# First block's down-projection of a hybrid encoder layer as seven block products, weight differences on GpSimd and activation sums by accumulating transfers

## The chip, the cores and the metric

The kernel runs on one core of a Trainium2 chip. A core has TensorE (PE; its weight loads are listed as PEld), VectorE (DVE), ScalarE (ACT), GpSimd (POOL), SyncE (SP), and 16 DMA engines that all queues share. The engines run side by side, each through its own instructions in a fixed order. The metric is the device time of one execution in microseconds (us); less is better.

## The reference

One layer of a streaming encoder over 2048 prompt rows and 128 sample rows of width 1024, all in fp32: a combined input projection, chunk-band attention and an mLSTM side by side (the mixers), an output projection with a residual, and then the part that the change touches, a feed-forward network with a causal depthwise convolution of width 3:

```python
def conv_ffn(h, buf, w_up, w_conv, b_conv, w_down):
    S = h.shape[1]
    u = h @ w_up
    ext = jnp.concatenate([buf.astype(u.dtype), u], axis=1)
    y = b_conv
    for j in range(CONV_W):
        y = y + ext[:, j:j + S] * w_conv[j]
    gate, up = jnp.split(y, 2, axis=-1)
    out = (jax.nn.gelu(gate, approximate=True) * up) @ w_down
    return out, ext[:, S:]

    ffn, new_buf = conv_ffn(rms_norm(x, norm_g[2]), conv_buf, w_up, w_conv, b_conv, w_down)
    x = x + rms_norm(ffn, norm_g[3])
```

`w_up` is 1024 x 5632, `w_down` 2816 x 1024. The 17 row tiles of 128 are the 16 of the prompt and one of the sample.

## The kernel before

**Numbers.** Every fp32 matrix is split into a high part that TensorE takes exactly and a remainder: ScalarE copies the high part (L1309), VectorE subtracts it (L1310), and `mm3` (L104 to L106) makes three matmuls, high by high, high by low, low by high.

**Stages.** The mixers come first: 14 groups of columns of the input projection for each of two halves of the rows (`seq`, `GROUPS`). Between the units of a group, a pump (`pump`) steps attention and mLSTM along. The output projection follows. Then the feed-forward network runs over three blocks of rows, `FBLOCKS`: six tiles, six tiles, five tiles. For each block the up-projection goes over 22 column pairs f (gate and up, 128 columns each), and then the down-projection over the same 22 f as its inner dimension.

**Up-projection.** It already runs as seven block products in place of eight (Strassen's scheme in Winograd's form), with sums of the weights and of the activations. For the first block the weight sums are made on the way: for each f, `load_quads` loads four quads of 128x512 (`wu`), VectorE makes four sums of them (`ws`, L1326), and GpSimd stores those to DRAM (`wsd`, L1328) for the later blocks. Quads are 11 tiles in rotation, so a new load by SyncE waits until an old quad has been split or stored. GpSimd also copies two columns of history into each `uu` or `ug` (from `halo`, L1495) and out of it (L1500), which the convolution on VectorE (L1504, L1505) reads. The result of one f, g (L1654), is gate times up for all rows of the block.

**Down-projection.** `FAST` names the blocks that take it as seven products, here the second and the third. Rows are paired (tiles 0 to 2 with 3 to 5), and so are f (f with f + 11, index k of 11) and the output columns (two halves of 512). `SEQUENCE` names for each product an activation sum (A11, A12, S2, S1, S3, S4, A22), a block or difference of the weights, and which of two sets of three accumulators it adds to. A product is 11 k x 3 tiles x 3 matmuls of 512 columns: 99. `store_a` makes the sums for those blocks: plain stores of A11, A12, A22; S1 by an accumulating transfer; S3, S2 and S4 by three subtractions on VectorE (L1597) and a store each. The weight differences (`wtd`) are made during the first block's down-projection: `folds`, stepped once per k, loads four quads of `w_down` on ScalarE's queue, subtracts four times on VectorE (L1181) and stores them through GpSimd (L1186).

The first block itself takes the plain way: g goes to DRAM (`gd`, L1662), and two passes, one per half of the output columns, each load 22 blocks of weights (`load_down`) and 22 of g, with six accumulators: 2 x 22 x 6 x 3 = 792 matmuls. Between the passes the accumulators are copied out (L1394). During either kind of down-projection the next block's activations are normalised, transposed (L1107) and summed.

**Order.** Each engine's order is fixed when the kernel is built, by a list scheduler with a timeline of its own. Instructions under `keep_in_program_order` hold their order among themselves.

## Time and profile before

| | |
|---|---|
| median of 3 runs | 2769.21 us (2767.95 to 2771.8) |
| the profiled execution | 2768.76 us |
| its span, first to last instruction | 2767.0 us |
| mean granted TensorE clock | 0.996 |
| mixers and output projection | 0 to 1315.9 us |
| first block: up, down | 321.9 us, 200.0 us |
| second block: up, down | 318.7 us, 173.6 us |

The page lists busy time by engine, the chain of work that ended last, and groups of instructions by source line; a group's row has its count, busy time, mean length in ns, and the idle time of its engine just before it with what ended that. Views of the trace give busy time in chosen stretches (the stretch, its length, busy time with the number of instructions for PE, PEld, DVE, ACT and POOL, then granted clock, DMA share and GB/s), waits (who waited for whom: total, times, longest), and single instructions in order of time (start, length, engine, line). In a view by tile or line the three lengths are minimum, median and maximum in ns. Line numbers are those of the kernel before; `wuh`, `wul` are the split weights, and an L with a number is a line.

### The profile page before, as it was taken

The page shows a single profiled execution, that of the slowest core. Times are in us where ns is not written, and L with a number is a line of the kernel's source. Part 1 is how long each engine was busy: PE and PEld are TensorE (multiplying, and loading weights), DVE is VectorE, ACT ScalarE, POOL GpSimd, SP SyncE. Part 2 cuts the span into 40 slices and gives each one's busy share as a digit, 9 for nine tenths or more (in the row PEclk, how much of TensorE's full clock was granted, in tenths as well). Part 3 has the DMA queues.
Part 4 walks back from the last instruction along what each step waited for, and adds up shares of the span by engine and source line. Part 5 has one row for each costly group of instructions (what it writes and reads, how often), then busy time and mean ns, then how long its engine had stood idle before and what let it go on. Part 6 is the DMA issues. An engine that isn't in the chain of part 4 may idle for free.

```text
span 2767.0 us, 47747 instructions
## 1 busy us (share of the span) xinstructions
PE 2693.8 (97%) x16422; PEld 2520.4 (91%) x16422; DVE 1943.2 (70%) x3615; ACT 1438.5 (52%) x2918; POOL 654.3 (24%) x1271
## 2 busy tenths in 40 slices
PE   8999999999999999999999999999999999999998
PEld 7899999998899998878999998789999878999976
DVE  5344455646546668766989987668888876998956
ACT  4355555645356666543545455445455665554554
POOL 1000010211100002344434322123332212455401
PEclk9999999999999999999999999999999999999999
DMA  5534355556554456355645559866785777787775
GB/s 184 158 116 139 105 161 173 158 155 210 166 180 143 140 168 195 108 167 196 229 153 187 168 189 326 300 222 205 230 239 174 248 235 231 222 257 230 247 261 178
DMA packets 326017, 536.11 MB, mean 194 GB/s; under 512 B 60002, under 2 KB 159806, under 8 KB 325646
## 3 DMA queue, kind: packets, MB, share of 16 engines
q1 hardware_dynamic: 248382, 393.82, 45.7%
q0 software_dynamic: 32464, 93.87, 10.4%
q10 hardware_dynamic: 44928, 45.37, 5.1%
q8 instruction: 129, 2.11, 0.3%
q14 instruction: 114, 0.93, 0.1%
HBM read 383.28 MB, written 159.08 MB: 196 GB/s over the span
## 4 chain that ended last, share of the span: by engine, by line
PE 53%; DVE 3%; DMA 2%; issue 1%; POOL 1%; ACT 1%; DVEq 0%; POOLq 0%; SPq 0%; ACTq 0%
PE uec L104 6%; PE uec L105 6%; PE uec L106 6%; PE dn L106 4%; PE dn L105 4%; PE dn L104 4%; PE ua L106 3%; PE ua L105 3%; PE ua L104 3%; PE wo L106 2%; PE wo L104 2%; PE wo L105 2%; PE dnm L106 2%; PE dnm L105 2%; PE dnm L104 2%
## 5 line engine op out<-in xcount | busy, mean ns | idle before, releaser
L104 PE MATMUL uec<-B,wuh 128*128 128x384 f32 (+1 forms) x720 | 236.1, 328 | 4.1 <-DVE uu L1644 4.1
L105 PE MATMUL uec<-B,wuh 128*128 128x384 f32 (+1 forms) x720 | 235.3, 327 | 0.0
L106 PE MATMUL uec<-B,wul 128*128 128x384 f32 (+1 forms) x720 | 234.1, 327 | 0.0
L1309 ACT CAST wuh<-wu 128x512 fp32r<-128x512 f32 x255 | 141.7, 618 | 108.8 <-PE uec L105 100.9
L1310 DVE TENSOR_TENSOR wul<-wu,wuh 128x512 fp32r<-128x512 f32 x255 | 165.5, 685 | 4.0 <-DMA x2d<-mx 2.8
L405 DVE CUSTOM_DVE_ANT_0 tmp<-s,nb 128x640 f32<-128x640 f32 (+4 forms) x128 | 94.4, 737 | 95.1 <-PE s L395 93.5
L104 PE MATMUL vo<-wi_h,hT 128*128 128x256 f32 x544 | 155.1, 285 | 0.6 <-DVE mt L211 0.6
L106 PE MATMUL vo<-wi_h,hT 128*128 128x256 f32 x544 | 155.6, 286 | 0.0
L105 PE MATMUL vo<-wi_l,hT 128*128 128x256 f32 x544 | 154.8, 285 | 0.0
L104 PEld LDWEIGHTS uec<-B,wuh 128*128 128x128 f32 x720 | 135.2, 188 | 6.6 <-DVE uu L1644 5.5
L104 PE MATMUL qk<-hT,wi_h 128*128 128x384 f32 (+1 forms) x384 | 128.5, 335 | 7.3 <-ACT qk_st L236 5.9
L105 PEld LDWEIGHTS uec<-B,wuh 128*128 128x128 f32 x720 | 135.4, 188 | 0.3
L106 PEld LDWEIGHTS uec<-B,wul 128*128 128x128 f32 x720 | 135.1, 188 | 0.0
L418 DVE TENSOR_TENSOR ptl<-pt,pth 128x640 fp32r<-128x640 f32 (+4 forms) x128 | 93.6, 737 | 55.9 <-ACT pth L417 54.8
L406 ACT ACTIVATE tmp<-tmp,mn 128x640 f32<-128x640 f32 (+4 forms) x128 | 97.6, 762 | 67.0 <-DVE mn L405 62.9
L1310 DVE TENSOR_TENSOR wdl<-wdr,wdh 128x512 fp32r<-128x512 f32 x198 | 125.1, 685 | 7.3 <-ACT wdh L1309 7.0
L1310 DVE TENSOR_TENSOR al<-ar,ah 128x768 fp32r<-128x768 f32 (+2 forms) x94 | 70.9, 764 | 82.5 <-ACT ah L1309 81.0
L105 PE MATMUL qb<-hT,wi_h 128*128 128x384 f32 (+1 forms) x384 | 127.9, 333 | 0.0
L105 PE MATMUL qk<-hT,wi_h 128*128 128x384 f32 (+1 forms) x384 | 127.5, 332 | 0.0
L106 PE MATMUL qk<-hT,wi_l 128*128 128x384 f32 (+1 forms) x384 | 127.2, 331 | 0.0
L106 PE MATMUL qb<-hT,wi_l 128*128 128x384 f32 (+1 forms) x384 | 127.2, 331 | 0.0
L104 PE MATMUL qb<-hT,wi_h 128*128 128x384 f32 (+1 forms) x384 | 127.1, 331 | 0.0
(445 smaller groups left out, 9373.0 us busy)
## 6 DMA issues: line engine op xcount, KB each, us to landing
wu<-in_w_up SPq DMA_DIRECT2D x220, 256.0 KB, 4.9
wu<-wsd SPq DMA_DIRECT2D x176, 256.0 KB, 4.8
wdr<-in_w_down SPq DMA_DIRECT2D x110, 256.0 KB, 5.0
wi_raw<-in_w_in SPq DMA_DIRECT2D x52, 512.0 KB, 4.0
wsd<-ws POOLq DMA_DIRECT2D x88, 256.0 KB, 3.6
wdr<-wtd SPq DMA_DIRECT2D x88, 256.0 KB, 5.3
gr<-gd SPq DMA_DIRECT2D x39, 384.0 KB, 6.0
kraw<-kTd SPq DMA_DIRECT2D x112, 128.0 KB, 3.2
```

The costliest lines, as they stand in the source:

```text
L104: nc.tensor.matmul(out, ah, bh, start=start, stop=False, skip_group_check=onto)
L105: nc.tensor.matmul(out, ah, bl, start=False, stop=False, skip_group_check=onto)
L106: nc.tensor.matmul(out, al, bh, start=False, stop=stop, skip_group_check=onto)
L405: nc.vector.tensor_tensor_reduce(o_, s_, b_, 1.0, 3e38, ALU.add, ALU.min, accum_out=mn)
L406: nc.scalar.activation(tmp[:, :n], tmp[:, :n], AF.Exp, bias=mn, scale=-1.0, accum_out=rsum[:, i % 4, hh:hh + 1])
L418: nc.vector.tensor_tensor(s.ptl[:, sl, qc], ptv, s.pth[:, sl, qc], op=ALU.subtract)
L1309: nc.scalar.copy(h, r)
L1310: nc.vector.tensor_tensor(l, r, h, op=ALU.subtract)
```

## The change

`FAST` takes in the first block, whose order of f becomes 0, 11, 1, 12 and so on. The weight differences must then be ready before its down-projection: `folds` now runs in the mixers, from the second group of the first half on, one step per unit, with loads, arithmetic and stores all on GpSimd. The signs of two differences are turned, and in the later blocks those of two sums with them.

The activation sums of the first block are not made on VectorE. `send_a` stores A11, A12, A22 and S1 as before, and makes S3, S2, S4 in DRAM, in one tensor with three slots (`sums`): ScalarE negates A21 (for f under 11) or A22, and GpSimd's queue stores the negated A21 into three slots, adds A11 to all three, the negated A22 to two and A12 to one. The steps for one f wait in the list `due` and are taken one per later f.

```diff
-FAST = (1, 2)
+FAST = (0, 1, 2)
+FOLD_AT = 1
...
+    sums = dt_([P, 3, NK, 384], "sums")
+    for i, what in enumerate(("S3", "S2", "S4")):
+        ad[0, what] = sums[:, i]
...
+                    keep(nc.gpsimd.dma_start(live[k, x], I["w_down"][k][:, x * 512:(x + 1) * 512]))
...
+        for k in range(NK):
+            load(k, (0, 1))
+            yield
+            load(k, (2, 3))
+            yield
+            yield
+            yield
             a, b, c, d = [live[k, x] for x in range(4)]
+            for o, x, y, op in ((a, b, a, ALU.subtract), (b, c, b, ALU.subtract), (c, a, c, ALU.subtract),
+                                (d, d, c, ALU.add)):
+                keep(nc.gpsimd.tensor_tensor(o, x, y, op=op))
                 yield
+            store(k, range(4))
+            yield
...
+            if half == 0 and gi >= FOLD_AT:
+                next(fold, None)
...
+        def next_due():
+            for step in due.pop(0) if due else ():
+                step()
+
+        def send_a(f, gt):
...
+            while len(due) < 4:
+                due.append([])
+            next_due()
+            neg = []
+
+            def negate():
+                neg.append(spare_tile(f"neg{b}_{f}")[:, :384])
+                keep(nc.scalar.activation(neg[0], gt[:, 384:768], AF.Copy, scale=-1.0))
+
+            def spread(src, lo, **how):
+                keep(send(sums[:, lo:3, k, :], src.unsqueeze(1).broadcast_to([P, 3 - lo, 384]), **how))
+
+            if f < NK:
+                send(ad[b, "A11"][:, k, :], gt[:, 0:384])
+                send(ad[b, "S1"][:, k, :], gt[:, 384:768])
+                due[0] += [negate, lambda: spread(neg[0], 0)]
+                due[1] += [lambda: spread(ad[b, "A11"][:, k, :], 0, accum_op=ALU.add)]
+            else:
+                send(ad[b, "A12"][:, k, :], gt[:, 0:384])
+                send(ad[b, "A22"][:, k, :], gt[:, 384:768])
+                send(ad[b, "S1"][:, k, :], gt[:, 384:768], accum_op=ALU.add)
+                due[0] += [negate]
+                due[1] += [lambda: spread(neg[0], 1, accum_op=ALU.add)]
+                due[2] += [lambda: spread(ad[b, "A12"][:, k, :], 2, accum_op=ALU.add)]
...
-            for o, x, y in ((s3, a11, a21), (s2, a22, s3), (s4, a12, s2)):
-                nc.vector.tensor_tensor(o, x, y, op=ALU.subtract)
+            for o, x, y, op in ((s3, a11, a21, ALU.subtract), (s2, s3, a22, ALU.subtract), (s4, a12, s2, ALU.add)):
+                nc.vector.tensor_tensor(o, x, y, op=op)
...
-                store_a(f, gt)
+                (store_a if b else send_a)(f, gt)
...
+        while due:
+            next_due()
...
-                    if b == 0:
-                        next(fold, None)
```

GpSimd early in the mixers, before: after the row scale of the last tile of the first half (n_16) come the masks of attention's bias (`nb`) and of the mLSTM (`mb`).

```order
L93 TENSOR_TENSOR n_16_rs<-n_16_ms,nhalf 128x1
L338 MEMSET nb_0_1243 64x64
L339 MEMSET nb_0_1243 64x64
L338 MEMSET nb_0_1314 64x64
L339 MEMSET nb_0_1314 64x64
```

The same place now (`fold` are the four quads of one k, here the second; `wtd`, the differences in DRAM, follow):

```order
L1185 DMA wtd_226<-fold_3_871 128x512
L1181 DMA fold_0_1093<-in_w_down 128x512
L1181 DMA fold_1_1095<-in_w_down 128x512
L1181 DMA fold_2_1130<-in_w_down 128x512
L1181 DMA fold_3_1132<-in_w_down 128x512
L1197 TENSOR_TENSOR fold_0_1093<-fold_1_1095,fold_0_1093 128x512
L1197 TENSOR_TENSOR fold_1_1095<-fold_2_1130,fold_1_1095 128x512
L1197 TENSOR_TENSOR fold_2_1130<-fold_0_1093,fold_2_1130 128x512
L1197 TENSOR_TENSOR fold_3_1132<-fold_3_1132,fold_2_1130 128x512
L342 MEMSET nb_0_1254 64x64
L343 MEMSET nb_0_1254 64x64
```

Two rounds of folds, each with four loads and four stores, now stand ahead of the first mask; the other nine come between later masks.

GpSimd in the first block's up-projection, before, around one f (`ws` are weight sums, `gd` the store of g):

```order
L1328 DMA wsd_257<-ws_2_16549 128x512
L1495 COPY uu_2_16624<-halo 128x2
L1328 DMA wsd_257<-ws_3_16550 128x512
L1500 COPY halo<-ug_1_16481 128x2
L1662 DMA gd_0_207<-g_0_16379 128x768
L1328 DMA wsd_258<-ws_0_16702 128x512
L1500 COPY halo<-uu_2_16624 128x2
```

And now (`y` holds g, `neg` its negated half; sums with 384 rows go to three slots):

```order
L1603 DMA sums<-ad_A_208 128x384
L1603 DMA sums<-ad_A_207 384x1x384
L1337 DMA wsd_251<-ws_1_17346 128x512
L1337 DMA wsd_251<-ws_2_17347 128x512
L1337 DMA wsd_251<-ws_3_17348 128x512
L1503 COPY uu_3_17422<-halo 128x2
L1337 DMA wsd_241<-ws_0_17502 128x512
L1508 COPY halo<-ug_13_17272 128x2
L1603 DMA sums<-neg_12_17171 128x2x384
L1337 DMA wsd_241<-ws_1_17503 128x512
L1606 DMA ad_A_207<-y_2_0_17163 128x384
L1607 DMA ad_S_210<-y_2_0_17163 128x384
```

Transfers into `sums` now stand between the stores of weight sums. The transfer of `neg_12` adds to the same k as that of `ad_A_207` six instructions ahead of it.

More of the change, by code (lines that the diff above doesn't have):

```diff
@@ L123, in hymba_step @@
     ad = {(b, what): dt_([P, NK, 256 if b == 2 and what in ("A22", "S2", "S3") else 384], f"ad{b}_{what}")
-          for b in FAST for what in ("A11", "A12", "A22", "S1", "S2", "S3", "S4")}
+          for b in FAST for what in ("A11", "A12", "A22", "S1", "S2", "S3", "S4") if b or what not in ("S2", "S3", "S4")}
+    sums = dt_([P, 3, NK, 384], "sums")
+    for i, what in enumerate(("S3", "S2", "S4")):
+        ad[0, what] = sums[:, i]
     wtd = [dt_([P, 2048], f"wtd{k}") for k in range(NK)]
@@ L1166, in late_B, with folds @@
             nc.vector.tensor_tensor(lo, lo.bitcast(F32), hi, op=ALU.subtract)
-    def folds(period, plan):
+    def folds():
+        keep = tc.keep_in_program_order
         live = {}
@@ L1237, in hymba_step @@
     chunks = []
+    fold = folds()
     norms = norm_steps(0)
@@ L1300, in hymba_step @@
                 mems.append(lambda i=i: mlstm_sample(i))
+    for _ in fold:
+        pass
     for cost in out:
@@ L1458, in hymba_step @@
     unfinished = []
-    fold = folds(4, {0: ("ab",), 1: ("cd",), 3: ("combine", "store")})
     def u_tile(name):
@@ L1883, in hymba_step @@
                     unfinished.append((tiles[j], rs))
-        if b == 0:
-            for _ in fold:
-                pass
         if not last:
```

22 lines of the change are left out of this document (6 added, 16 removed).

## The prediction

> **What bounds the kernel now.** First the page's head and its chain of waits, then busy time by stage.
>
> ```profile
> span 2767.0 us, 47747 instructions
> PE 2693.8 (97%) x16422; PEld 2520.4 (91%) x16422; DVE 1943.2 (70%) x3615; ACT 1438.5 (52%) x2918; POOL 654.3 (24%) x1271
> PE 53%; DVE 3%; DMA 2%; issue 1%; POOL 1%; ACT 1%; DVEq 0%; POOLq 0%; SPq 0%; ACTq 0%
> ```
>
> TensorE sets the end: it is busy for 97% of the span and leads the chain. So only fewer or shorter matmuls help, and every new wait that reaches TensorE costs. The next rows are busy time in four stretches: up-projection of the first block, its down-projection, up-projection of the second block, its down-projection. The second block's down-projection already runs as seven products, so the trace holds the shape that the first block is to take. Below them stand the matmuls into the two kinds of accumulator (dn, dnm) and the transposes for the next block, in the two down stretches.
>
> ```profile
> 1315.90:1637.80 321.90, 319.44 (x1825) 316.88 (x1824) 299.13 (x451) 166.34 (x267) 118.30 (x190) 1.00 0.53 180
> 1637.80:1837.80 200.00, 194.27 (x867) 157.68 (x866) 138.82 (x199) 93.93 (x158) 39.15 (x75) 1.00 0.85 289
> 1837.80:2156.50 318.70, 318.17 (x1826) 317.69 (x1824) 268.91 (x410) 162.60 (x272) 109.23 (x207) 1.00 0.71 212
> 2156.50:2330.10 173.60, 171.94 (x768) 138.76 (x769) 124.49 (x187) 109.01 (x200) 30.96 (x45) 1.00 0.75 247
> ...
> 1637.80:1837.80 200.00, 136.40 (x528) 98.99 (x528) 3.26 (x5) 0.00 (x0) 1.00 0.85 289
> 2156.50:2330.10 173.60, 129.39 (x462) 85.74 (x462) 3.85 (x6) 3.21 (x6) 1.00 0.75 247
> ...
> 1637.80:1837.80 200.00, 75.69 (x264) 48.73 (x264) 1.28 (x2) 0.00 (x0) 1.00 0.85 289
> 2156.50:2330.10 173.60, 73.89 (x231) 43.61 (x231) 2.04 (x3) 1.79 (x3) 1.00 0.75 247
> ...
> 1637.80:1837.80 200.00, 7.59 (x48) 5.87 (x48) 7.98 (x12) 6.77 (x12) 1.00 0.85 289
> 2156.50:2330.10 173.60, 6.81 (x48) 5.08 (x48) 6.99 (x12) 6.03 (x12) 1.00 0.75 247
> ```
>
> Columns: stretch, us, then busy PE, PEld, DVE, ACT, POOL, granted clock, DMA share, GB/s. The first block has 528 + 264 = 792 matmuls and 200.0 us, the second 462 + 231 = 693 and 173.6 us, with 48 transposes each.
>
> **Part 1: 99 matmuls fewer.** The timeline of TensorE in the second block's down stretch has 31 matmuls of 512 columns from the first row here to the last:
>
> ```profile
> 2221.59 0.39 PE L104 MATMUL dn<-wdh,ah 128*128 128x512 f32 x1
> ...
> 2228.55 0.40 PE L106 MATMUL dnm<-wdh,al 128*128 128x512 f32 x1
> ```
>
> (2228.55 − 2221.59) / 30 = 0.232 us each, so 99 × 0.232 = 23.0 us. The stretches differ by more, 200.0 − 173.6 = 26.4 us, since TensorE idles 5.7 us in the first and 1.7 in the second. Part of that idle time is the change from the first half of the output columns to the second, where a late weight load and the evacuations stand on the chain:
>
> ```profile
> 1738.57 5.98 DMA wdr<-in_w_down
> 1744.57 0.63 ACT wdh L1309
> 1747.64 1.28 DVE fr L1394 x2
> ```
>
> Seven products have no such turn: two sets of three accumulators alternate. Bounds −23.0 and −26.4; I take −25.5, nearer to the whole stretch, because that is the same code on the same shapes. VectorE gets lighter too, so it is no new bound:
>
> ```profile
> L1181 DVE TENSOR_TENSOR fold<-fold,fold 128x512 f32<-128x512 f32 x44 | 30.2, 686 | 1.9 <-DMA fold<-in_w_down 1.7
> L1310 DVE TENSOR_TENSOR wdl<-wdr,wdh 128x512 fp32r<-128x512 f32 x198 | 125.1, 685 | 7.3 <-ACT wdh L1309 7.0
> ```
>
> The 44 folds (30.2 us) leave, 77 − 44 = 33 more weight splits at 0.685 (22.6) come.
>
> **Part 2: weight differences by GpSimd, in the mixers.** Per k: four loads that were on ScalarE's queue and now go through GpSimd's, four subtractions or additions, four stores; eleven k, from the second projection group on. GpSimd's nearest arithmetic is the residual addition of twice the width, beside it a VectorE instruction that met it:
>
> ```profile
> L1039 POOL TENSOR_TENSOR mx<-mx 128x1024 f32<-128x1024 f32 x17 | 41.0, 2410 | 2.5 <-DVE mx L1038 2.5
> L1099 DVE SCALAR_TENSOR_TENSOR x2r<-x2r,n_rs,g x17: 1277/1285/3400, 1211.1 to 2264.6; 128x1024 f32<-128x1024 f32 x17
> 1234.27 2.38 POOL L1039 TENSOR_TENSOR mx<-mx 128x1024 f32<-128x1024 f32 x1
> 1234.33 3.40 DVE L1099 SCALAR_TENSOR_TENSOR x2r<-x2r,n_rs,g 128x1024 f32<-128x1024 f32 x1 [0.71 <-POOL n_rs L93]
> 130.00:200.00 70.00, 70.00 (x492) 69.62 (x491) 32.42 (x70) 34.52 (x78) 0.58 (x4) 1.00 0.39 116
> 200.00:270.00 70.00, 70.00 (x480) 69.54 (x479) 34.70 (x70) 36.00 (x81) 0.40 (x3) 1.00 0.44 132
> 270.00:340.00 70.00, 70.00 (x521) 69.73 (x520) 32.32 (x73) 36.46 (x86) 0.29 (x2) 1.00 0.37 114
> ```
>
> Half of 2.410 is 1.205 us, times 44 = 53 us of GpSimd time in stretches where it is busy 0.3 to 0.6 of 70 us. The cost is what VectorE loses: an instruction of 1.28 us took 3.40 when GpSimd's began just before it, so it was held for GpSimd's whole length. VectorE is busy 32.3 to 34.7 of 70 us (46 to 50%), so about 53 × 0.46 = 24 us at the most of holds. TensorE had no idle time in these stretches, so VectorE's results came early enough; how early the trace does not say. Bounds 0 and +24; I take +2, because holds of at most 1.2 us are spread over hundreds of us and VectorE has over half its time free. If that cover were gone, the attention's evacuations would be late next.
>
> The Trainium skill (GPSIMD Engine Reference, section "Engine selection") speaks against this move: two-input elementwise work belongs on VectorE, GpSimd being about half as fast. The rows agree (1.205 against 0.686 us). It names also the shared SBUF interfaces (section "Key points"), which is the hold above; by it this part would cost its upper bound, and the first rival prices that.
>
> What waits behind the folds in GpSimd's queue are the masks of attention's bias (nb) and of the mLSTM. The first mask was set at 70.46 us and the first score matmul started at 91.3:
>
> ```profile
> fold<-in_w_down ACTq DMA_DIRECT2D x44, 256.0 KB, 5.7
> 70.46 0.14 POOL L338 MEMSET nb<- 64x64 f32 x1 [27.01 <-DMA nb<-relrow]
> L394 PE MATMUL s<-kh,qs x224: 221/309/524, 91.3 to 1178.1; 128*128 128x320 f32 x96, 128*128 128x128 f32 x8, 128*128 128x384 f32 x8
> ```
>
> Some 20 us of slack cover one k of folds (loads land in 5.7 us by the first row here, four operations take 4.8): nothing.
>
> **Part 3: activation sums by accumulating transfers, in the up stretch.** One store per f goes (gd). Per pair of f come: four plain stores, one accumulating store (S1), a negated store to three slots, and accumulating ones to three, two and one. VectorE gets nothing; ScalarE gets 22 negations of about 0.48 us (its 128x384 copy), 10.5 us on 166.34 of 321.90: covered. GpSimd's issue costs:
>
> ```profile
> L1662 POOL DMA_DIRECT2D gd<-g x22: 539/539/614, 1356.3 to 1659.6; - x22
> L1590 POOL DMA_DIRECT2D ad_S<-y x11: 882/917/948, 1882.1 to 2181.1; - x11
> L1619 ACT COPY x<-ua 128x384 f32<-128x384 f32 x44 | 21.0, 477 | 25.5 <-PE ua L106 25.4
> ```
>
> Plain 0.54, accumulating 0.92 us, for 128 rows. With no price for 256 or 384 rows, the bounds are the same price and two or three times it. Per pair: 4 × 0.54 + 0.92 − 2 × 0.54 = 2.0, and the sums 0.54 + 3 × 0.92 = 3.3 up to 3 × 0.54 + 6 × 0.92 = 7.1. Times 11: 58 to 100 us on GpSimd's 118.30 of 321.90, so it stays under 70%. The danger is who waits for it. In this stretch VectorE is busy 299.13 of 321.90 us and has 22.8 to give. It waits for weight loads already, and those sit in tiles that GpSimd's stores free:
>
> ```profile
> SPq L1321 <- DMA wsd<-ws: 15.5, 4, 5.9
> DVE ws L1326 <- DMA wu<-in_w_up: 3.8, 7, 1.2
> DVE uu L1484 <- POOL ug L1495: 0.4, 1, 0.4
> ```
>
> Traffic: ten more units of 196.6 KB per k are written, 21.6 MB in 322 us, 67 GB/s on 180. The second block's up stretch had 212 GB/s, share 0.71, accumulating stores too, and lost 0.5 us of TensorE; the first's down stretch stood at 0.85. Bounds 0 (as in the second block) and +43 (second rival). I take +2, nearer the stretch of the same shape.
>
> **Sum.** 2767.0 − 25.5 + 2 + 2 = 2745.5 us of span. The profiled execution took 2768.76, 1.8 above its span, and the median shown is 2769.21, 0.45 above that: 2745.5 + 2.2 = 2748 us.
>
> **Rivals.** First, the mixers pay: VectorE's holds reach TensorE. For it: the 3.40 us row. Against: no TensorE idle from 130 to 340 us. Half of 24 us exposed gives 2745.5 − 2 + 12 + 2.2 = 2758; all of it, 2770.
>
> Second, slower: GpSimd stands at an accumulation that must wait for the one before it to land, and the stores of weight sums behind it free their tiles late; the next weight loads are late, then VectorE, then TensorE. A like wait exists in the second block's up stretch:
>
> ```profile
> POOL out_y_prompt L1433 <- DMA x2d<-f: 27.2, 6, 5.8
> ```
>
> It was up to 5.8 us and cost TensorE nothing there, with VectorE at 84%. Here the steps on one k are issued one f apart, 321.90 / 22 = 14.6 us, which should cover the landing. If instead two waits of 3 us fall in each of 11 pairs, GpSimd stands 66 us; all of it passed to VectorE, less its 22.8 free, is 43 us: 2745.5 − 2 + 43 + 2.2 = 2789. It decides against the change once VectorE is held over 22.8 + 23.5 = 46 us, 2.1 per f; half-way to that, it takes part of the gain (2755 to 2765).
>
> The Trainium skill (DMA: Bandwidth & Descriptors, section "Rules for kernel authors") says that an accumulating transfer reads its destination and writes it later, so the earlier one's completion must be waited for. That is the wait in the row above; it gives this rival its mechanism, not its size.
>
> Third, the change doesn't do what it says: seven products in the first block wait for loads, and the stretch stays near 200 us: 2745.5 + 25.5 + 2.2 = 2773. Against it: the second block moved 247 GB/s so and idled 1.7 us.
>
> **How the numbers follow.** Forecast 0.64 (its own range 2740 to 2756), mixers 0.13, GpSimd's waits 0.18, no shortening 0.05. About 0.2% (5.5 us) is what a measurement tells from no change, so faster means under 2763.7. Faster: 0.64 + 0.10 + 0.07 = 0.81; same: 0.03 + 0.03 + 0.05 = 0.11; slower: 0.08, all from the second rival. Range 2739 to 2766: it takes in the half-exposed mixers and leaves out about 0.17 above and a little below.
>
> **What would show it.** Down stretch of the first block: 693 matmuls, 173 to 177 us, no fold on VectorE. Mixers: fold instructions on GpSimd near 1.2 us, TensorE idle up by under 5 us before 500. Up stretch: 322 to 327 us, GpSimd busy 177 to 219, VectorE's wait for wu loads under 15 us. I am wrong if VectorE's or TensorE's waits there grow beyond that, if issues of 384 rows cost over 3 us, or if the down stretch keeps its 200 us.

## The result and the profile after

The change is slower.

| | before | the change |
|---|---|---|
| median, runs | 2769.59 us (2767.95 to 2771.8), 4 | 2800.64 us (2798.85 to 2803.05), 4 |
| ratio, 95% interval | 1 | 1.011 [1.0094, 1.0126] |
| span of the profiled execution | 2767.0 us | 2797.1 us |
| mixers and output projection | 1315.9 us | 1345.7 us (+29.8) |
| first block, up | 322.0 us | 352.0 us (+30.0) |
| first block down and second block up together | 518.6 us | 495.5 us (−23.1) |
| the rest | 610.5 us | 603.9 us (−6.6) |

The stages are counted from the first matmul of one to the first of the next (`ua` starts an up-projection, `dn` or `dnm` a down-projection). The first block's down stretch and the next up stretch stand together because the prediction drew the line between them where the down-projection's last matmul ends, some 6 us before the next `ua`. The rest, from the second block's down-projection on, runs the same code but for turned signs; over the seventeen kernels other than the kernel before it took 603.9 to 611.7 us, so its −6.6 is no gain of the change.

First the page's first lines and its chain shares, for the change:

```profile
span 2797.1 us, 47840 instructions
PE 2689.8 (96%) x16323; PEld 2510.9 (90%) x16323; DVE 1943.6 (69%) x3599; ACT 1463.6 (52%) x2983; POOL 792.8 (28%) x1436
PE 36%; DMA 3%; DVE 2%; issue 1%; ACT 1%; POOL 0%; DVEq 0%; POOLq 0%; SPq 0%; ACTq 0%
```

99 matmuls are gone (16422 to 16323), yet TensorE is busy only 4 us less (2693.8 to 2689.8): part of what is left runs at a lower clock (0.99 in the first two stretches below). Then busy time in stretches, for the change: up to the first up-projection, first up, first down, second up.

```profile
0.00:1345.60 1345.60, 1285.89 (x8703) 1211.62 (x8704) 776.44 (x1700) 672.24 (x1606) 301.29 (x557) 0.99 0.57 173
1345.60:1697.70 352.10, 328.14 (x1825) 320.87 (x1825) 299.25 (x452) 174.05 (x286) 162.51 (x256) 0.99 0.78 216
1697.70:1873.00 175.30, 171.17 (x759) 137.74 (x759) 127.34 (x186) 112.86 (x205) 34.43 (x51) 1.00 0.84 261
1873.00:2193.00 320.00, 319.69 (x1832) 319.05 (x1830) 266.99 (x406) 162.65 (x270) 104.86 (x197) 1.00 0.71 207
```

The down stretch does what was forecast: 175.3 us where 200.0 stood. The two stretches ahead of it pay more than that. In the up stretch TensorE idles 352.1 − 328.1 = 24.0 us, where it idled 2.5, and needs 8.7 us more for the same 1825 matmuls.

**The up stretch.** Waits of VectorE and of SyncE's queue there, for the change:

```profile
DVE ws L1335 <- DMA wu<-in_w_up: 34.6, 9, 5.8
...
SPq L1330 <- DMA wu<-in_w_up: 35.9, 4, 11.2
...
SPq L1330 <- DMA wsd<-ws: 29.5, 7, 8.0
```

What TensorE waits for there ends the chain:

```profile
PE uec L105 <- DVE ug L1492: 11.4, 5, 4.2
PE uec L105 <- DVE uu L1492: 5.8, 3, 2.3
PE uec L105 <- DVE uu L1686: 5.0, 3, 1.7
```

VectorE waits 34.6 us for loads of the up-projection's weight, 3.8 before, and it had 22.8 to spare. TensorE waits 22.2 us for VectorE's tiles at `uec`, 0.3 before. In order of time VectorE's waits come in pieces of up to 5.8 us, such as these:

```profile
1515.89 0.69 DVE L1335 TENSOR_TENSOR ws<-wu,wu 128x512 f32<-128x512 f32 x1 [5.25 <-DMA wu<-in_w_up]
...
1551.93 0.69 DVE L1335 TENSOR_TENSOR ws<-wu,wu 128x512 f32<-128x512 f32 x1 [5.38 <-DMA wu<-in_w_up]
```

They wait for `wu` loads. Transfers issued between 1490 and 1556 us in the change, with KB each and the median us to landing:

```profile
wu<-in_w_up SPq DMA_DIRECT2D x15, 256.0 KB, 10.1
...
sums<-ad_A POOLq DMA_DIRECT2D x2, 576.0 KB, 10.9
```

The 576 KB transfer adds A11, read from DRAM, onto three slots in DRAM; such a transfer to several slots is called a spread below. The trace gives the landing of 20 of the stretch's `wu` loads. The 8 issued while a spread from A11 was on its way landed in 7.8 to 11.6 us (median 10.2), the 12 others in 3.7 to 5.9 (median 4.9), those beside other transfers into `sums` among them.

GpSimd's queue over the whole up stretch (packets, MB, share of the 16 DMA engines, called transfer engines below), before and then in the change:

```profile
q0 software_dynamic: 8320, 29.89, 24.0%
```

```profile
q0 software_dynamic: 19252, 48.03, 52.7%
```

Before, 24.0% of 321.9 us are 77.3 us for 29.89 MB, 2.6 us for each MB. The change adds 18.1 MB, and they take 52.7% of 352.1 − 77.3 = 108.3 us, 6.0 for each.

**The mixers.** The folds run from 44 to 416 us. Stretches from 40 to 240 and 240 to 440, before and then in the change:

```profile
40.00:240.00 200.00, 190.62 (x1247) 186.18 (x1246) 82.63 (x215) 84.62 (x195) 3.20 (x13) 0.99 0.45 133
240.00:440.00 200.00, 198.65 (x1473) 194.94 (x1472) 101.18 (x241) 102.80 (x249) 10.62 (x35) 1.00 0.48 145
```

```profile
40.00:240.00 200.00, 185.52 (x1192) 180.87 (x1191) 85.69 (x208) 79.95 (x187) 62.60 (x87) 0.97 0.67 196
240.00:440.00 200.00, 189.05 (x1357) 184.39 (x1356) 100.36 (x218) 95.45 (x229) 57.74 (x92) 0.99 0.57 176
```

TensorE gets through 1192 + 1357 = 2549 instructions where it did 2720; the transfer share went up by half in the first. One place, read in order of time, shows one way in which time is lost. ScalarE, VectorE and TensorE in the change (start, length, engine, line, then in brackets the wait ahead):

```profile
64.36 0.49 ACT L242 ACTIVATE qk_st<-qk 128x384 f32<-128x384 f32 x1 [4.13 <-DMA out_v_sample<-va_st]
68.01 1.14 ACT L1223 CAST wi_h<-wi_raw 128x512 fp32r<-128x512 f32 x2 [3.16 <-DMA wi_raw<-in_w_in]
...
68.66 0.77 DVE L1224 TENSOR_TENSOR wi_l<-wi_raw,wi_h 128x512 fp32r<-128x512 f32 x1 [5.51 <-ACT wi_h L1223]
...
75.05 0.97 ACT L636 ACTIVATE pks<-pks 4x128 f32<-4x128 f32 x3 [5.51 <-DMA qTd<-qk_st]
...
76.07 0.33 PE L77 MATMUL pkTs<-ident,pks 128*128 128x128 f32 x1 [2.65 <-ACT pks L636]
```

A store and a weight load are late, so ScalarE's cast is (68.0; 62.3 before), VectorE's next split with it, the gate arithmetic queued behind that split on VectorE, and TensorE stands 2.65 us at the transpose of `pks`. (ScalarE's row for `pks` names a transfer; VectorE's write of that tile ends at 75.02 us, 0.03 ahead of ScalarE's start.) Before, it ran straight on:

```profile
62.31 0.62 ACT L1219 CAST wi_h<-wi_raw 128x512 fp32r<-128x512 f32 x1 [1.11 <-DMA wi_raw<-in_w_in]
...
72.33 0.27 PE L76 MATMUL pkTs<-ident,pks 128*128 128x128 f32 x1
```

The stop costs twice. Stretches in the change, ahead of the wait and just after it (granted clock, transfer share and GB/s are the last three):

```profile
60.00:73.00 13.00, 13.00 (x77) 12.43 (x76) 6.97 (x25) 2.25 (x5) 5.91 (x4) 1.00 0.98 292
77.20:80.00 2.80, 2.80 (x10) 2.76 (x10) 0.48 (x2) 0.00 (x0) 1.59 (x3) 0.50 1.02 367
```

For these 2.8 us the clock is at 0.50, and TensorE does 10 instructions where some 16 fit (77 in 13.0 us ahead). The trace's record of the clock has such drops of 3.4 us each: six in the change's mixers and three in its first up stretch, one and none before, three and none in the program without folds (4). At half clock the nine lose some 9 × 3.4 / 2 = 15 us, 5 of them in the up stretch.

### The profile page after: what moved, and what is told of

It reads as the page before. It is cut to its first block, busy times and chain, and to the rows that moved or that the text cites. A ratio compares the mean times of both kernels' runs of the same rounds, so it can differ in the third digit from the quotient of the medians.

```text
span 2797.1 us, 47840 instructions
## 1 busy us (share of the span) xinstructions
PE 2689.8 (96%) x16323; PEld 2510.9 (90%) x16323; DVE 1943.6 (69%) x3599; ACT 1463.6 (52%) x2983; POOL 792.8 (28%) x1436
## 5 line engine op out<-in xcount | busy, mean ns | idle before, releaser
L105 PE MATMUL uec<-B,wuh 128*128 128x384 f32 (+1 forms) x720 | 236.9, 329 | 26.0 <-DVE ug L1492 11.2
L105 PE MATMUL dn<-wdh,ah 128*128 128x512 f32 x462 | 183.4, 397 | 6.8 <-ACT ah L1318 6.0
L1319 DVE TENSOR_TENSOR al<-ar,ah 128x768 fp32r<-128x768 f32 (+2 forms) x141 | 108.5, 778 | 116.3 <-ACT ah L1318 112.9
L107 PE MATMUL dn<-wdh,al 128*128 128x512 f32 x462 | 185.7, 402 | 2.9 <-DVE al L1319 2.7
L106 PE MATMUL dn<-wdl,ah 128*128 128x512 f32 x462 | 182.9, 396 | 0.6 <-DVE wdl L1319 0.5
L1318 ACT CAST ah<-ar 128x768 fp32r<-128x768 f32 (+2 forms) x141 | 96.1, 692 | 152.7 <-PE dnm L106 114.4
L1319 DVE TENSOR_TENSOR wdl<-wdr,wdh 128x512 fp32r<-128x512 f32 x231 | 145.3, 683 | 7.4 <-ACT wdh L1318 7.2
L105 PE MATMUL qk<-hT,wi_h 128*128 128x384 f32 (+1 forms) x384 | 130.0, 338 | 3.6 <-ACT qk_st L242 3.0
L1318 ACT CAST wdh<-wdr 128x512 fp32r<-128x512 f32 x231 | 127.3, 619 | 11.7 <-issue 3.8
```

The costliest lines, as they stand in the source:

```text
L105: nc.tensor.matmul(out, ah, bh, start=start, stop=False, skip_group_check=onto)
L106: nc.tensor.matmul(out, ah, bl, start=False, stop=False, skip_group_check=onto)
L107: nc.tensor.matmul(out, al, bh, start=False, stop=stop, skip_group_check=onto)
L1318: nc.scalar.copy(h, r)
L1319: nc.vector.tensor_tensor(l, r, h, op=ALU.subtract)
```

## The experiments

Sixteen kernels ran, each compared with runs of the kernel before made on the same chip; the chips differ between groups of kernels, so kernels are compared with each other by their ratios. "Mixers" and "up" below are lengths of stages in the one profiled execution, counted as above. Six programs in which the mixers are the change's own, or differ by doubled operations alone (it, that one, and four below that alter only the feed-forward part), had 1333 to 1346 us there, and two others whose mixers are the same, transfers without arithmetic (3 and 5), had 1325.6 and 1339.1. So a difference of ten us in that stage needs the ratios. Where it matters, a second thing is given: how many of TensorE's 16,323 instructions in the trace stand over 20 places from where they stand in the program without folds (4), matched by source line, tiles and shape. For the change it is 49, with the folds' operations on VectorE 90, so there TensorE's order is the same for practical purposes.

**1. Each part alone.** The folds alone:

```diff
-FAST = (0, 1, 2)
+FAST = (1, 2)
```

> The weight differences by GpSimd in the mixers alone: the first block stays with eight plain products, so no accumulating transfers, no negations; the down-projection has no fold work either. If the mixers' loss belongs to the folds alone (main theory): mixers and output projection 1340 to 1350 us as in the change (1345.6; 1315.9 before), first block's up stretch back at 320 to 325, its down stretch 197 to 200, median 2795 to 2800. If the two losses hang together (the rival: the loss in the mixers comes from the changed order of the whole program, not from the folds): mixers near 1316 and a median near 2768.

2790.23 us, ratio 1.0094 [1.0059, 1.013]; mixers 1338.1, up 322.3, first down and second up 518.8. The median is 5 us under the forecast, as the mixers are 2 under theirs. The mixers' loss belongs to the folds, and the up stretch is whole again. The rival, a changed order, falls for TensorE: of its 8,703 instructions in the mixers 5 stand over 20 places from where they stood before, here as in the change.

The sums by VectorE:

```diff
-                (store_a if b else send_a)(f, gt)
+                store_a(f, gt)
```

> The change with the first block's S2, S3 and S4 made as the second block makes them: three VectorE subtractions and three plain stores for each pair, no transfer from DRAM to DRAM but the one accumulation onto S1, no negation. If the three-slot accumulating transfers take the up stretch's time (main theory): up stretch 320 to 326 us (352.1 in the change, 320.0 in the second block, which works so), waits of the VectorE weight sums for wu under 10 us, median 2768 to 2775. If it is VectorE or the write traffic of the stores as such: 335 to 352, median 2785 to 2800. The mixers stay at 1340 to 1350 by both.

2769.19 us, 1.0018 [1.0000, 1.0035]; mixers 1335.8, up 328.0, first down and second up 492.9. The up stretch and VectorE's wait for `wu` in this kernel:

```profile
1335.80:1663.80 328.00, 322.15 (x1825) 316.51 (x1823) 315.34 (x486) 167.99 (x268) 173.22 (x251) 1.00 0.62 201
```

```profile
DVE ws L1332 <- DMA wu<-in_w_up: 5.3, 7, 1.1
```

33 subtractions more on VectorE (96% busy) cost 6 us; the accumulating spreads had cost 30. The 328 lies 2 over the forecast's top: VectorE is busy 315.3 us of it. The mixers lie 4 under the 1340 to 1350 expected.

**2. What of the spreads is dear.** As plain writes, and then without those that read DRAM:

```diff
-                due[1] += [lambda: spread(ad[b, "A11"][:, k, :], 0, accum_op=ALU.add)]
+                due[1] += [lambda: spread(ad[b, "A11"][:, k, :], 0)]
...
-                due[1] += [lambda: spread(neg[0], 1, accum_op=ALU.add)]
-                due[2] += [lambda: spread(ad[b, "A12"][:, k, :], 2, accum_op=ALU.add)]
+                due[1] += [lambda: spread(neg[0], 1)]
+                due[2] += [lambda: spread(ad[b, "A12"][:, k, :], 2)]
```

> The change with the spreads onto the three sums as plain writes: same sources, same places, same sizes, same order on GpSimd's queue, but nothing is added (left out of the computation: the additions in S2, S3 and S4, which hold the last value written). If the accumulation itself is dear (theory P): up stretch 322 to 332 us (352 in the change, 328 with the sums on VectorE), the 576 KB transfers from A11 land in about half of the 9 to 13 us seen, median 2770 to 2780. If it is the bytes and the read from DRAM (theory Q): 342 to 354, median 2790 to 2801.

```diff
-                due[1] += [lambda: spread(ad[b, "A11"][:, k, :], 0, accum_op=ALU.add)]
...
-                due[2] += [lambda: spread(ad[b, "A12"][:, k, :], 2, accum_op=ALU.add)]
```

> The change without the two spreads that read DRAM (A11 onto three sums, 576 KB, and A12 onto one, 192 KB, for each pair); the negations and their two spreads stay, one of them accumulating (left out of the computation: A11 and A12 in S2, S3 and S4). If the long transfers from DRAM to DRAM hold the wu loads back (main theory): up stretch 326 to 335 us, waits of the VectorE weight sums for wu under 15 us (34.6 in the change), median 2772 to 2782. If the accumulating two-slot transfer from SBUF does as much (rival): 338 to 346.

Plain: 2774.43 us, 1.0026 [1.0008, 1.0043], up 334.5. Without the DRAM reads: 2771.76 us, 1.0016 [1.0002, 1.0030], up 321.3. The up stretch with plain spreads, its queue and its spreads from A11:

```profile
1333.10:1667.60 334.50, 322.34 (x1825) 316.64 (x1824) 299.15 (x451) 173.61 (x286) 151.72 (x256) 1.00 0.70 228
```

```profile
q0 software_dynamic: 14903, 48.09, 43.2%
...
sums<-ad_A POOLq DMA_DIRECT2D x9, 576.0 KB, 6.9
```

In the change the same transfers read:

```profile
sums<-ad_A POOLq DMA_DIRECT2D x9, 576.0 KB, 11.2
```

The bytes are the same, 48.1 MB, the instructions and their order too. With accumulation there are 4,300 packets more, a spread lands in 11.2 in place of 6.9 us, and the stage takes 17.5 us more. So 17.5 of the 30 us are the accumulating, and 12.5 the plain traffic and the negations that came with it (334.5 against 322.0). By the ratios, 1.0110 and 1.0026, the accumulating costs 0.84%, some 23 us of the whole. Plain misses its range by 2.5 us. Without the two spreads that read DRAM the loss is gone, although an accumulating one from SBUF stays; that stage came out 5 below its forecast.

```profile
DVE ws L1335 <- DMA wu<-in_w_up: 5.3, 5, 1.6
```

That is VectorE's wait for `wu` in that kernel: 5.3 us, near the 3.8 before. The landings of `wu` loads show the same (20 known in each):

| | issued while a spread from A11 is on its way | the others |
|---|---|---|
| the change | 8: 7.8 to 11.6 us, median 10.2 | 12: 3.7 to 5.9, median 4.9 |
| plain spreads | 7: 5.6 to 9.7, median 7.5 | 13: 2.9 to 5.1, median 3.2 |
| without spreads from DRAM | none | 20: 3.0 to 6.2, median 4.7 |

So a load of 256 KB beside a 576 KB transfer from DRAM to DRAM is late, whether that one adds or not; adding keeps it on its way for 11.2 in place of 6.9 us and makes the loads beside it later still.

**3. What of the folds is dear, first tries.** On the whole change: GpSimd's 44 operations left out (so the products that need the differences compute with others), put on VectorE, doubled.

```diff
-                keep(nc.gpsimd.tensor_tensor(o, x, y, op=op))
```

> The change without the 44 GpSimd subtractions and additions of the folds; their loads and stores stay on GpSimd's queue (left out of the computation: the weight differences, so the three products that use them multiply by plain blocks). If GpSimd's arithmetic holds VectorE and thereby TensorE (theory A): mixers 1316 to 1325 us, median 2772 to 2780. If the 23 MB of fold transfers crowd the mixers' own loads (theory B): mixers 1335 to 1346, median 2790 to 2800. The up stretch stays at 350 to 354.

```diff
-                keep(nc.gpsimd.tensor_tensor(o, x, y, op=op))
+                keep(nc.vector.tensor_tensor(o, x, y, op=op))
```

> The change with the folds' 44 operations on VectorE in place of GpSimd, at the same places; transfers unchanged. By theory A (holds by GpSimd) the mixers fall to 1318 to 1328 us, as 44 x about 0.6 us find room on a VectorE that is under 60 per cent busy there; median 2773 to 2782. By theory B (transfers) they stay at 1335 to 1346, median 2790 to 2800.

```diff
-                keep(nc.gpsimd.tensor_tensor(o, x, y, op=op))
+                for _ in range(2):
+                    keep(nc.gpsimd.tensor_tensor(o, x, y, op=op))
```

> The change with each of the folds' 44 GpSimd operations issued twice, one right after the other; transfers unchanged (changed in the computation: the second issue works on the first's result, so the weight differences are others). If GpSimd's arithmetic is what delays VectorE (theory A: 44 operations gave 11 to 20 us): mixers 1355 to 1368 us (1345.7 in the change), median 2810 to 2822. If it is the transfers and the order (theory B): within 5 us of the change, 1340 to 1351, median 2796 to 2806.

Left out: 2789.86 us, 1.0091 [1.0062, 1.0120], mixers 1325.6 in an execution 9.5 us under that kernel's median. On VectorE: 2787.8 us, 1.0084 [1.0054, 1.0115], mixers 1326.5. Doubled: 2800.97 us, 1.0118 [1.0101, 1.0136], mixers 1339.2. Against the change's 1.0110 [1.0094, 1.0126] the first two gain 0.19% and 0.26%, 5 and 7 us, with intervals that overlap the change's: the mixers stand near what theory A asked, the medians between the theories or at the edge of theory B's. The third shows no price of a second helping. So neither theory was shown, and the place was still open.

**4. Other places and paces for the folds.** All with the sums by VectorE and the folds' arithmetic by VectorE, the first in the second half of the mixers:

```diff
-            if half == 0 and gi >= FOLD_AT:
+            if half == 1 and gi >= FOLD_AT:
```

with `FOLD_AT = 2`.

> A version meant to keep the gain and drop both losses: seven products in the first block, its sums S2, S3 and S4 by VectorE, the folds' arithmetic on VectorE, and the folds put in the second half of the mixers (from its third group on), where VectorE is about 60 per cent busy and the masks and first loads are done. If the mixers' loss came from GpSimd's arithmetic and from transfers in the crowded first 450 us: mixers 1316 to 1326 us, up 326 to 330, first down 173 to 178, median 2748 to 2758, ratio 0.994 to 0.997. If fold transfers cost about 10 us wherever they are (rival): mixers 1326 to 1336, median 2760 to 2768, ratio 0.998 to 1.001.

2782.65 us, 1.0051 [1.0033, 1.0069], mixers 1356.5: a miss on the wrong side. The stretch from 640 to 840 us, where the folds now fell (698 to 922), in this kernel and then before:

```profile
640.00:840.00 200.00, 177.43 (x1166) 164.76 (x1164) 112.07 (x268) 82.16 (x197) 56.39 (x127) 0.97 0.79 249
```

```profile
640.00:840.00 200.00, 191.22 (x1297) 179.52 (x1296) 104.73 (x259) 92.58 (x220) 18.17 (x57) 1.00 0.59 178
```

VectorE does the arithmetic, and TensorE loses 14 us here at a transfer share of 0.79. Here 2,724 of TensorE's instructions have moved, so not all of it need be the transfers.

No folds at all, and three paces with loads and stores on ScalarE's queue:

```diff
-    fold = folds()
+    fold = iter([])
...
-        src = I["w_down"][k] if blk < 4 else wtd[k]
+        src = I["w_down"][k]
```

> Seven products in the first block, its sums by VectorE, and no folds at all: neither loads, arithmetic nor stores of weight differences (left out of the computation: the three products that use differences read plain blocks of the weight, so the down-projections load as many bytes as before). The ceiling of what a better placing of the folds can give. If the mixers' loss is all the folds': mixers 1314 to 1320 us, up 326 to 330, first down 173 to 177, median 2745 to 2752, ratio 0.991 to 0.995. If part of it is the changed program order: mixers above 1325, median 2757 or more.

```diff
-                    keep(nc.gpsimd.dma_start(live[k, x], I["w_down"][k][:, x * 512:(x + 1) * 512]))
+                    keep(nc.scalar.dma_start(live[k, x], I["w_down"][k][:, x * 512:(x + 1) * 512]))
...
-                keep(nc.gpsimd.dma_start(wtd[k][:, x * 512:(x + 1) * 512], live.pop((k, x))))
+                keep(nc.scalar.dma_start(wtd[k][:, x * 512:(x + 1) * 512], live.pop((k, x))))
...
-            if half == 0 and gi >= FOLD_AT:
+            if (half or gi >= FOLD_AT) and u % 3 == 0:
```

(the last two lines as for every third unit; every second has `u % 2`, every unit leaves that line as in the change.)

> Sums by VectorE as above; the folds at the change's pace (a step at every unit from the first half's second group), with loads and stores on ScalarE's queue and the arithmetic on VectorE, so that nothing of the folds stands on GpSimd. If bursts of fold transfers delay the mixers' own loads (theory B, as the trace of the change shows at 64 to 76 us): all 23 MB fall in some 250 us, mixers 1328 to 1350, median 2758 to 2780. If GpSimd's queue or arithmetic was the cause (theory A): mixers 1316 to 1322, median 2747 to 2754.

> As the one before with a fold step at every second unit, so that the 23 MB spread over about 600 us. By theory B: mixers 1320 to 1330 us, median 2750 to 2762, faster than with a step at every unit. By theory A as at every unit: 1316 to 1322.

> As the one before with a fold step at every third unit, over about 800 us. By theory B: mixers 1318 to 1326 us, median 2748 to 2758, ratio 0.993 to 0.997, the best of the three paces, unless the transfers in the crowded stretch from 500 to 800 us (transfer share 0.6) cost what the slower pace gains. By theory A the three paces agree within 5 us.

| | median | ratio | mixers |
|---|---|---|---|
| no folds | 2750.79 us | 0.9939 [0.9921, 0.9958] | 1322.9 us |
| every unit | 2779.18 us | 1.0047 [1.0031, 1.0063] | 1346.2 us |
| every second | 2781.7 us | 1.0064 [1.0042, 1.0085] | 1351.9 us |
| every third | 2797.63 us | 1.0106 [1.0089, 1.0124] | 1366.8 us |

The median of the ceiling is where it was expected, 15.6 us under the 2766.35 us of the kernel before in those runs. Its mixers, 7 us over those of the kernel before, lie between the two ranges. TensorE's order there is that of the kernel before (none of 8,703 instructions moved), so the 7 us are not its order. The paces go against theory B as it was put: every second unit is no better than every unit, and every third is the worst. But in these three TensorE's order changed as well (2,856, 1,169 and 3,655 instructions moved) and ScalarE now stands at transfers, so they don't tell pace from order. What they tell is that this was no way out.

**5. The parts of the folds, each alone, on one order.** On the sums by VectorE, where TensorE's order is that of the program without folds (0 and 16 instructions moved): arithmetic on four tiles that stay, with the plain blocks read as in the program without folds (that line is not shown again), and then transfers without arithmetic.

```diff
-                    live[k, x] = spare_tile(f"fold{k}_{x}")
-                    keep(nc.gpsimd.dma_start(live[k, x], I["w_down"][k][:, x * 512:(x + 1) * 512]))
+                    if k == 0:
+                        live[x] = spare_tile(f"fold{x}")
+                        keep(nc.gpsimd.memset(live[x], 0.0))
+                    live[k, x] = live[x]
...
-                keep(nc.gpsimd.dma_start(wtd[k][:, x * 512:(x + 1) * 512], live.pop((k, x))))
+                live.pop((k, x))
```

> The sums by VectorE; of the folds only GpSimd's 44 operations, on four tiles that stay where they are: no loads and no stores (left out of the computation: the weight differences; the products read plain blocks of the weight instead). Without folds this program takes 2750.8 us (mixers 1322.9), with them 2769.2 (1335.8). If GpSimd's arithmetic costs by holding VectorE: median 2759 to 2766, VectorE's subtractions of 512 columns in the mixers lengthened from about 0.69 us as with the folds. If the transfers cost: 2749 to 2754, mixers 1318 to 1325.

```diff
-                keep(nc.gpsimd.tensor_tensor(o, x, y, op=op))
```

> The sums by VectorE; of the folds only the loads and stores on GpSimd's queue, no arithmetic (left out of the computation: the weight differences, so that the products which use them read plain blocks). If the transfers cost: median 2762 to 2770, mixers 1331 to 1340, ScalarE's wait for wi_raw between 40 and 440 us 25 to 30 us as in the change (11.7 before). If GpSimd's arithmetic costs: 2752 to 2758, mixers 1322 to 1328. If each costs half: 2758 to 2763.

| folds | median | ratio | mixers |
|---|---|---|---|
| none | 2750.79 us | 0.9939 [0.9921, 0.9958] | 1322.9 us |
| GpSimd's arithmetic alone | 2751.39 us | 0.9954 [0.9939, 0.9969] | 1324.0 us |
| transfers alone | 2762.57 us | 0.9985 [0.9973, 0.9997] | 1339.1 us |
| both | 2769.19 us | 1.0018 [1.0000, 1.0035] | 1335.8 us |

The arithmetic alone, 0.15% over none, is not told from nothing. The transfers alone cost 0.46% of 2766 us, 12 to 13 us; their 2762.57 us lie in the range for the transfers and also, at its top, in that for half each. Both cost 0.79%, 22 us.

As TensorE's order is the same in all of these, the start of its n-th instruction tells where the time goes (us, one execution each):

| | 800th | 2000th | 3000th | 8000th |
|---|---|---|---|---|
| before | 139.5 | 313.2 | 450.8 | 1171.1 |
| no folds | 138.9 | 312.6 | 451.3 | 1178.1 |
| GpSimd's arithmetic alone | 140.0 | 313.7 | 454.0 | 1179.2 |
| transfers alone | 142.9 | 326.9 | 470.8 | 1192.7 |
| both | 146.9 | 323.5 | 470.6 | 1190.9 |
| the change | 148.3 | 325.4 | 473.4 | 1199.3 |

By the 3000th, when the folds are over, the transfers alone have cost 20 us and the change 23, the arithmetic alone 3. The 7 us that the change loses after that are lost without folds too, so of its +29.8 us in the mixers some 23 are the folds'. Between two executions of these mixers there are 10 us: the first try without arithmetic (3) stands at 461.0 at the 3000th.

GpSimd does hold VectorE, though. VectorE's splits of `wi` between 40 and 420 us before, and then with the arithmetic alone, with a group beside them that reads PSUM:

```profile
L405 DVE CUSTOM_DVE_ANT_0 tmp<-s,nb 128x640 f32<-128x640 f32 (+4 forms) x48 | 31.5, 655 | 66.2 <-PE s L395 64.9 <-issue 1.1
...
L1220 DVE TENSOR_TENSOR wi_l<-wi_raw,wi_h 128x512 fp32r<-128x512 f32 x44 | 28.9, 692 | 24.5 <-ACT wi_h L1219 23.8 <-DMA kTd<-qk_st 0.7
```

```profile
L1223 DVE TENSOR_TENSOR wi_l<-wi_raw,wi_h 128x512 fp32r<-128x512 f32 x44 | 32.9, 783 | 23.6 <-ACT wi_h L1222 23.5
L406 DVE CUSTOM_DVE_ANT_0 tmp<-s,nb 128x640 f32<-128x640 f32 (+4 forms) x48 | 31.4, 654 | 63.8 <-PE s L396 63.7
```

The splits' mean grows from 692 to 783 ns, 4 us on 44. The median is 686 in both: four of the 44 took 1.58 to 1.79 us, each while a fold operation ran on GpSimd, so they were held some 1 us. TensorE's waits name no `wi_l` in either. The forecast of ScalarE's wait for `wi_raw` with the transfers alone was 25 to 30 us, and it is 18.6 (11.7 before): the stage lost what was expected, so other places must have a part in it.

**6. A version that keeps the gain.** Both edits that gained, the sums and the folds' arithmetic on VectorE:

```diff
-                (store_a if b else send_a)(f, gt)
+                store_a(f, gt)
...
-                keep(nc.gpsimd.tensor_tensor(o, x, y, op=op))
+                keep(nc.vector.tensor_tensor(o, x, y, op=op))
```

> The sums by VectorE and the folds' arithmetic by VectorE, fold transfers on GpSimd's queue at the change's places: the two edits that each gained on their own, together. If they add up: mixers 1322 to 1330 us, up 326 to 330, first down 172 to 177, median 2753 to 2760, ratio 0.995 to 0.998. If GpSimd's arithmetic is not what cost (transfers alone): median 2765 to 2771, as with the folds on GpSimd.

and with `FOLD_AT = 4`:

> The first of these four with the folds begun three groups later (from the fifth group of the first half), so that they miss the crowded stretch from 45 to 115 us, where the masks and the first attention loads come. If that stretch is where the fold transfers cost: mixers 1318 to 1325 us, median 2749 to 2756. If they cost wherever they are: within 4 us of the first of these four, or more where they reach the stretch from 500 us on.

The first: 2759.03 us, 0.9976 [0.9964, 0.9987], mixers 1328.3, up 328.1, first down and second up 493.3. That is as forecast for gains that add up, and under the 2765 to 2771 us forecast for GpSimd's arithmetic costing nothing. It beats the kernel before by 0.24%. The second: 2774.57 us, 1.0032 [1.0018, 1.0045], mixers 1345.7. Missing the crowded stretch was worse, not better: its folds went into the stretch from 208 to 578 us. Stretches from 240 to 440 in the first and the second:

```profile
240.00:440.00 200.00, 195.82 (x1423) 190.43 (x1422) 109.09 (x250) 97.80 (x238) 34.71 (x76) 1.00 0.61 191
```

```profile
240.00:440.00 200.00, 188.75 (x1357) 183.66 (x1356) 104.56 (x237) 93.01 (x226) 35.82 (x83) 0.98 0.62 193
```

The transfer share is the same, 0.61 and 0.62, and TensorE's loss is 7 us apart. So the share alone doesn't set the price. That it is set by which small loads are hit is likely and not shown.

## Why the prediction was wrong

The forecast was 2748 us, in a range of 2739 to 2766; the change takes 2800.64. The sum's first term was right and its other two were far too small. With VectorE's sums in place of the spreads and without the folds the kernel takes 2750.79 us, so the forecast comes near a change that has neither.

**Part 1, 99 matmuls fewer: right.** The down stretch took 175.3 us, forecast 173 to 177. First down and second up lost 23.1 us together, at the edge of the bounds, and 24.2 to 28.2 in the kernels with seven products and without accumulating spreads, up to 2 beyond the other bound. The third rival falls.

**Part 2, the folds in the mixers: the step that failed is its list of costs.** It took +2 from holds of VectorE and priced the rest at nothing. The mechanism that it priced is real and small: an operation of the folds took 1257 to 1747 ns with a median of 1.29 us, forecast 1.205; four of 44 splits were held some 1 us; alone that costs nothing that can be told. The term that is missing is the transfers. The 44 loads and 44 stores of 256 KB are 23 MB. In the kernel before, they lay in the first down stretch, where the transfer share was 0.85 and TensorE idled 5.7 us in all; in the mixers they raise the share from 0.45 to 0.67 and from 0.48 to 0.57. The prediction read "TensorE had no idle time in these stretches" as results that come early enough. It does not say how early, and TensorE had no idle time there to take up a late load. Alone the transfers cost 12 to 13 us, with GpSimd's arithmetic 22. In the one place read in order of time the loss goes through a load of `wi_raw`, a split, the arithmetic queued behind it, and a drop of the clock after it. That the masks' 20 us of slack cover a fold holds for the first mask (70.46 us before, 75.24 now); the second came at 92.68 in place of 71.69 us, behind a second round, and the first score matmul at 102.9 in place of 91.3. "TensorE idle up by under 5 us before 500" was wrong: it idles 36.2 us there, 21.9 before, and 59.7 up to the first up-projection, 43.8 before.

The first rival named the right stage with the wrong cause, and its price was 10 to 22 us for holds.

**Part 3, the sums by accumulating transfers: the step that failed is the traffic's price.** The prediction counted 21.6 MB at the same price as all others and compared with the second block's up stretch, share 0.71, which lost nothing; it took +2 and bounded +43. It measured +30. 18.1 MB cost 6.0 us of transfer engines for each MB, not 2.6 (as plain writes 3.7), and 17.5 us of the loss come from accumulating alone. The like stretch was not alike: the second block's accumulating stores are of 192 KB from SBUF; here are spreads of 576 KB from DRAM to DRAM. GpSimd's own price was below its lower bound: busy 162.5 us of 352, forecast 177 to 219, with issues into `sums` at 1.0 us (plain and accumulating from `neg`) and 1.2 us (from DRAM) at the median.

The second rival had the right sign, the right chain at its far end (`wu` late, then VectorE, then TensorE) and a size not far off (43 for 30). Its cause is not what happened. By it GpSimd stands at an accumulation that waits for the one before. What GpSimd waits for at the spreads in the change, up to 1760 us, is mostly ScalarE:

```profile
POOL sums L1603 <- ACT neg L1600: 18.2, 11, 5.9
POOL sums L1603 <- DMA sums<-neg: 11.5, 2, 7.5
```

Both waits for a transfer come after the up stretch has ended. With plain spreads the same order stands on GpSimd, and the stage is 17.5 us shorter. The stores of weight sums did free tiles later (SyncE waits 29.5 us for them, 15.5 before), but as they land in 5.0 us in place of 3.5. And the loads themselves are slow while a spread from DRAM to DRAM is on its way.

**What stays open.** Whether GpSimd's arithmetic costs anything on top of the transfers: by the ratios 0.33% and 0.42% (transfers alone and with VectorE's arithmetic, against both on GpSimd), 0.15% alone, 0.08% for a second helping, each give or take some 0.2%. So the first two differ from nothing, by little, and that they differ from the last two is not shown. With VectorE's arithmetic the stores start at 73.8 us and the second round of loads after them; with GpSimd's the stores start at 55.3 and the second round's loads at 57.5, into a stretch with the transfer share at 0.98. That the arithmetic acts by this timing is argued, not shown. Late masks are no likelier: with the operations doubled the first score matmul came at 114.3 us, and that kernel is no slower than the change. And it is open why the folds are cheap between 44 and 407 us and dear between 187 and 578.

## What to carry to other kernels

Count a moved step's bytes as well as its instructions, and price them where they land: a stage in which TensorE never waits has no slack that the trace shows, and here 23 MB cost more (0.46%) than the arithmetic that they fed (0.15%, not told from nothing). A transfer that accumulates from DRAM to DRAM is not a free adder: ask how long it is on its way, and which small load on the path is issued meanwhile. Before a whole change is kept or dropped, undo its parts one at a time: here one part was worth 16 us (0.9939), under two others that took some 47 (1.0110 against 0.9939).

## What the runs showed that was not expected

- An accumulating spread of 576 KB from DRAM landed in 11.2 us at the median, the same spread as a plain write in 6.9, and GpSimd's queue took 52.7% of 16 transfer engines against 43.2% for the same 48 MB. A 256 KB load issued meanwhile landed in 10.2 or 7.5 us, in place of 4.9 or 3.2.
- After TensorE had stood 2.65 us its granted clock was 0.50 for 3.4 us (76.9 to 80.3), some 1.7 us lost again. One stop of 1.81 us was followed by the same drop at 1206.7 us.
- GpSimd's arithmetic held four of 44 of VectorE's subtractions from SBUF (0.69 us, then 1.58 to 1.79) and left the mean of those on scores in PSUM alone (655 and 654 ns).
- The same 23 MB cost 0.37% or 0.93% of the whole, some 10 or 26 us (0.9976 and 1.0032 against 0.9939), by their place, with VectorE's arithmetic and nearly the same order on TensorE (46 and 520 instructions moved).
